# A two-layer hybrid decoder on one core: beta and alpha in fp32 on four column groups, paired small products, a fourth output tile ahead

## The chip, the core and the metric

The kernel runs on one core of one Trainium2 chip. The time is the device time of one execution in microseconds (us); the kernel before has a median of 2566.28 us over three runs (2564.98 to 2567.65). TensorE does matmuls and transposes and is called PE, VectorE is DVE, ScalarE is ACT, GpSimd is POOL, and SyncE (SP) issues the DMAs.

## The reference

The input x is 1024 tokens by 1024 channels in fp32. Two residual layers follow each other, each with a token mixer and a SwiGLU FFN, and a last RMSNorm. Cut to what matters here:

```python
def mixer_ab(h, ...):                     # layer 0
    qkv, z, beta_raw, alpha_raw, gate_b, gate_c, sc_in = split_cols(h @ w_in, AB_SPLITS)
    qkv = silu(causal_depthwise_conv(qkv, conv_w))
    beta = sigmoid(beta_raw)              # 4 heads
    g = -exp(a_log) * softplus(alpha_raw + dt_bias)
    o_a = gated_delta_rule(q, k, v, g, beta)      # chunked, triangular solve
    ...
def mixer_cd(h, ...):                     # layer 1
    o_c = hgrn2_recurrence(silu(hq), k_in, hi, log_f)    # chunked, per-channel decay
    for p, (window, dilation) in enumerate(((128, 1), (512, 4), (2048, 16))):
        o_p, lse_p = dilated_window_attention(sq[p], sk[p], sv[p], window, dilation)
    o_d = softmax-over-p weighted sum of o_p
    return concatenate([o_c, o_d]) @ w_out

for layer in range(2):
    h = h + mixer(rms_norm(h, norm_mix_g[layer]))
    h = h + (silu(hn @ w_gate) * (hn @ w_up)) @ w_down   # hn = rms_norm(h, norm_ffn_g)
return rms_norm(h, norm_final_g)
```

Beta and alpha are eight columns of `w_in` (four heads each), in the kernel the input `w_ba`.

## The kernel before

The state lies transposed: channels on the 128 partitions, 512 tokens (one of two halves) along the free side, so a tile of 128 channels by 512 tokens fills one PSUM bank. Three kinds of PSUM tiles share the eight banks: `psg` (2), `psu` (3) and `psm` (3). A dense product in fp32 accuracy is made from fp32r parts: `split` makes a high part on ACT and the rest on DVE, and `mm3` (L126 to L128) issues three matmuls for each block of 128 input channels: high by high, high by low, low by high. These three lines are most of the program; `hnh` and `hnl` are the two parts of the normed state, `w` the split weights in a ring of four units, loaded by `wload` through the tile `raw`.

The norm needs the mean square of each token. `tr.squares` and `tr.piece` make and add the squares (ACT and POOL, L183 and L187, name `acc`), `rms` sums them over partitions with small matmuls against ones (L199), and `spread` transposes the result over all partitions (L213). In layer 0 the projections run ahead of the norm: the matmuls use x times the norm gain, and each product is multiplied by `rb` (the spread reciprocal root) when it leaves PSUM (`lead`, L1208). Their order at the start is written by hand (`ordered` is a manual schedule for PE, DVE and ACT). After `ordered.close()` a list scheduler with priorities sets the order of each engine.

The rest of layer 0's first stage goes through eight units `u` (four heads by two halves). Between the four projections of a unit, `step(u, i)` runs one piece of other work as the string `plan[u]` says: `S` the next part of `scalars()`, `A` the first and `B` the second part of `chunk_mats` of an earlier unit, `x` nothing. Units without an entry use `"AxBx"`. `scalars()` makes beta and alpha: the raw weights `w_ba` are split into 16 fp32r columns, 32 matmuls (L1259) multiply them with `hnh` and `hnl`, DVE scales by `rb` into `bat` (L1262), and small matmuls with a selection matrix (`sel16`, L1264) add high and low parts and turn tokens onto partitions. Then follow the gates' cumulated sums and factors (`sca`). `chunk_mats` makes key by key and key by query products (L1429) and transposes (`nn`, L1442).

Layer 1's mixer is driven by two generators, `hg_chain` (HGRN2, eight units of `hgrn`) and `loc` (the attention). `tick(cost)` is called between the dense matmuls; it adds cost to what is due and runs a step of each when one is due. PE's and DVE's order is here the order of these calls. `hgrn` computes products inside chunks level by level; `blocks` (L1805) does the small levels in 32-wide column groups, L1855 the level of 32 and L1860 the level of 64, from `ms[3]` in two 64-wide groups.

A step of the attention (`local`) does the scores of step n, the flip (transpose of the exponentials, so that keys are on partitions) of step n−1 and the outputs of step n−2. For the third dilation (`self.p == 2`) a stream has only 64 positions; its scores (L2099) are 64-wide, DVE's reduce adds the mask and finds the maximum (L2106), ACT takes exponentials (L2107), the flip is L2113 into `dp` (two tiles, `diag`), the outputs L2139. `combine` weighs the three dilations on ACT and DVE (L2219, name `ol`), transposes on PE (L2226), and stores to `cat`, from where `joined` loads and splits it for the output projection.

`leading` computes parts of the first output tiles (input blocks 0 to 5 of 8) ahead, while the last attention steps run; `out_proj` finishes them, adds to the residual `h`, calls `tr.piece` for the next norm, and stores by `tr.save`.

Of the kernel before, what the change touches and what calls it, by code (L numbers as in the profile page):

```python
# [54 lines left out]
def hybrid_trunk_kernel(ctx: ExitStack, tc: tile.TileContext, x_t, w_all, w_down, w_ba, vecs, c_f, c_i, c_rope, out):  # L55
# [23 lines left out]
    dia32 = cf[:, C_DIA:C_DIA + 32]  # L79
    sel16 = cf[:16, C_SEL:C_SEL + 8]  # L80
    swam = cf[:, C_SWA:C_SWA + 256]
# [1079 lines left out]
    def out_proj(name, cat_d, tr, src, order, half, hp, lead=None):  # L1161
# [4 lines left out]
        for d0 in range(0, KT, 2):  # L1166
            w = ws.get(d0) or wload((name, d0), (name, d0 + 1))
            if d0 + 2 < KT:
                tr.load(half, src, range(d0 + 2, d0 + 4))
            for i in range(2):  # L1170
                if d0 + i in banks:
                    o = proj(wk(w, i), qs, rest, banks.pop(d0 + i), first=False)
                else:
                    o = proj(wk(w, i), qs, order, psg() if i else psu())
                h = tr.at(half, d0 + i)
                V.tensor_tensor(h, h, o, op=ADD)
                tr.piece(half, d0 + i)
                tr.save(half, d0 + i, hd[2 * layer][half])
                yield


    def mixer_ab(hn, rb, hp, tr, first, second, close):
        scr_n = dr.tile([4, 32, 32, 32], F32, name="scr_n")
# [27 lines left out]
        early = {}  # L1211
        a, b = range(KH), range(KH, KT)
        os3 = [proj(wk(wqk, i), hn[0], a, last=False) for i in range(2)]
        for i in range(2):
            proj(wk(wqk, i), hn[0], b, os3[i], first=False)
        os3.append(proj(wk(wvz, 0), hn[0], a, last=False))
        r = tr.rms(0)
# [6 lines left out]
        for which, o in enumerate(os3):  # L1224
            early[0, which] = lead(o, 0)
        second(1)
        early[1, 0] = proj(wk(wqk, 0), hn[1])
        early[1, 1] = proj(wk(wqk, 1), hn[1])
        second(2)
        early[1, 2] = proj(wk(wvz, 0), hn[1])  # L1230
        second(3)
        ordered.close()
        close()
        with ExitStack() as es:
# [8 lines left out]
            sca = {n: keep.tile([P, 8, 4], F32, name="s_" + n) for n in sc_names}  # L1243
            raw = fp.tile([P, KT, 8], F32, name="wba_raw")
            dma(raw, w_ba)
            na = keep.tile([P, 4], F32, name="na")
            wba = keep.tile([P, KT, 16], F32R, name="wba")
            split(wba[:, :, 0:8], wba[:, :, 8:16], raw)

            def scalars():  # L1250
                with ExitStack() as e2:
# [3 lines left out]
                    for half in range(NH):  # L1255
                        o = psu()
                        for k in range(KT):
                            for j in range(2):
                                T.matmul(o[:16, :], wba[:, k, :], hk(hn[half], j, k),  # L1259
                                         start=k == 0 and j == 0, stop=k == KT - 1 and j == 1)  # L1260
                        bat = bp.tile([16, HT], F32, tag="bat", name="bat", bufs=1)
                        V.tensor_tensor(bat, o[:16, :], rb[half][:16, :], op=MULT)  # L1262
                        for tt in range(4):
                            T.matmul(sel[:, half * 32 + tt * 8:half * 32 + tt * 8 + 8], bat[:, tt * P:(tt + 1) * P],  # L1264
                                     sel16, start=True, stop=True)
                    V.tensor_copy(ba, sel[:, 0:64].rearrange("p (c e) -> p c e", c=8))
# [95 lines left out]
            if True:  # L1362
# [84 lines left out]

                plan = {1: "xSSS", 2: "ABAB"}
                units, sc_ = [], scalars()
# [282 lines left out]
    def mixer_cd(hn, hp, pairs):  # L1732
# [7 lines left out]
        with ExitStack() as es:  # L1740
# [67 lines left out]
            def hgrn(u, states, ending):  # L1808
# [49 lines left out]
                for c in range(4):  # L1858
                    r, z = c % 2 * 64, 3 * P + c // 2 * 64
                    T.matmul(od[r:r + 64, z:z + 64], m[:, c * P:c * P + 64], m[:, c * P + 64:(c + 1) * P],  # L1860
                             start=True, stop=True, tile_position=(0, r))
                kt = hl("e4", (4, P), 3)
# [75 lines left out]
            def leading(tick):  # L1938
# [6 lines left out]
                ws[2] = wload(("cdo", 2), ("cdo", 3))  # L1945
                for d, bank in ((0, psg), (1, psg), (2, psu)):
                    o = banks[d] = bank()
                    for ks in ((0, 1), (2, 3), (4, 5)):
                        proj(wk(ws[d // 2 * 2], d % 2), qs, ks, o, first=ks[0] == 0, last=False)
                        tick(0.5)  # L1950
                while len(whole) < 4:
# [57 lines left out]
            class Attend:  # L2009
# [82 lines left out]

                def short_scores(self, n):
                    o = psm()
                    for b in range(2):
                        for e in range(2):
                            i = (2 * n + b) * 2 + e
                            t = slice(i * 32, (i + 1) * 32)
                            T.matmul(o[e * 64:(e + 1) * 64, (b + e) % 2 * 64:(b + e) % 2 * 64 + 64],  # L2099
                                     self.q.rearrange("p b t -> p (b t)")[:, i * 64:(i + 1) * 64],  # L2100
                                     self.k[:, :, t], start=True, stop=True, tile_position=(0, e * 64))
                    s = self.sc[n] = tl("sc", bufs=2)
                    for x in range(2):
                        z = slice(x * 64, (x + 1) * 64)
# [4 lines left out]

                def short_flip(self, n):  # L2110
                    s = self.sc.pop(n)
                    o = psm()
                    T.transpose(o[:, 0:P], s[:, 0:P], ident)  # L2113
                    pt = self.pt[n] = diag[n % 2]
                    copy = V.tensor_copy if n % 2 else S.copy
                    copy(pt[0:64, 0:256].rearrange("p (a t) -> p a t", t=64)[:, 0::3],
                         o[0:64, 0:P].rearrange("p (a t) -> p a t", t=64))
                    copy(pt[64:128, 128:192], o[64:128, 0:64])
                    copy(pt[64:128, 64:128], o[64:128, 64:128])

# [10 lines left out]

                def outputs(self, n):
                    pt = self.pt.pop(n)
                    if n % 2 == 0:
# [255 lines left out]
    tr.load(0, x_t[0], range(4, KT))  # L2390
    dma(cf[:, 0:P], c_f[:, 0:P])
    o = psg()
    for _ in range(16):
# [12 lines left out]
    for i in range(2):  # L2406
        arrived_half(i, *w1)
        for d in range(4 + 2 * i, 6 + 2 * i):
            scaled_in(0, d)
    w0, w1 = coming(("ab", 8)), coming(("ab", 12))  # L2410
    ring.tile([P, 24], F32, name="pad")
# [30 lines left out]
    for layer in range(2):  # L2442

        if layer == 0:
            mixer_ab(hn, rb, hp, tr, first, second, es.close)
        else:
# [63 lines left out]
def shape_constants():  # L2510
# [6 lines left out]
    cf[:, C_DIA:C_DIA + 32] = (i % 32)[:, None] == np.arange(32)[None, :]  # L2517
    cf[0:8, C_SEL:C_SEL + 8] = np.eye(8)
    cf[8:16, C_SEL:C_SEL + 8] = np.eye(8)
    cf[:, C_SWA:C_SWA + P] = np.where(i[None, :] >= i[:, None], 0.0, NEG)  # L2520
# [67 lines left out]
```

## Time and profile before

| | before |
|---|---|
| median of three runs | 2566.28 us (2564.98 to 2567.65) |
| profiled execution | 2559.81 us, span 2558.0 us |
| mean granted clock of PE | 0.997 |
| PE busy | 2537.2 us, 99% |
| DVE, ACT, POOL busy | 65%, 40%, 22% |
| share of PE in the chain that ended last | 71% |

The span goes from the first to the last instruction of the profiled execution, which took 1.8 us longer in all and is 6.5 us under the median. A matmul of 512 fp32r columns shows a duration near 0.39 us but starts every 0.227 us, since matmuls overlap in the pipeline; costs on PE are therefore read from start to start.

### The profile page before, as it was taken

The numbers are of one execution on the slowest core, as the hardware profiler recorded it, in microseconds if no ns is written. First come the engines' busy times: TensorE is split into PE (matmuls) and PEld (weight loads), VectorE is DVE, ScalarE is ACT, GpSimd is POOL, SyncE is SP. The second block draws the span as 40 slices with busy tenths as digits, with TensorE's granted clock in tenths as the row PEclk, the third lists the DMA queues.
The fourth block names the chain that finished last, engine by engine and source line by source line (L and its number), as shares of the span: only waits on it lengthen the run. The fifth ranks groups of instructions, "written<-read, shape, count | busy, mean of one in ns | idle before, by whom it ended". The sixth has DMA issues, their size and how long they took to land.

```text
span 2558.0 us, 37563 instructions
## 1 busy us (share of the span) xinstructions
PE 2537.2 (99%) x14076; PEld 2114.1 (83%) x14076; DVE 1661.4 (65%) x2819; ACT 1033.9 (40%) x1861; POOL 557.5 (22%) x461
## 2 busy tenths in 40 slices
PE   9999999999999999999999999999999999999998
PEld 7788888888888888887888888888888888888887
DVE  7886776685655665568677657655658565666554
ACT  5432123343333345344433446565535333334442
POOL 1110111334333310033333100000033333330001
PEclk9999999999999999999999999999999999999999
DMA  3434446424556588544234456767752455568853
GB/s 137 150 99 152 127 141 206 173 81 168 174 195 207 202 289 307 177 155 152 107 110 138 166 154 198 205 181 208 223 173 87 166 189 192 201 219 289 271 178 119
DMA packets 270070, 451.82 MB, mean 177 GB/s; under 512 B 33824, under 2 KB 125760, under 8 KB 269760
## 3 DMA queue, kind: packets, MB, share of 16 engines
q1 hardware_dynamic: 269888, 449.43, 53.9%
q8 instruction: 110, 1.80, 0.3%
q14 instruction: 72, 0.59, 0.1%
HBM read 307.16 MB, written 142.16 MB: 176 GB/s over the span
## 4 chain that ended last, share of the span: by engine, by line
PE 71%; DVE 7%; DMA 2%; ACT 1%; issue 1%; SPq 0%; POOL 0%; DVEq 0%; ACTq 0%; POOLq 0%
PE psu L126 12%; PE psu L128 12%; PE psu L127 12%; PE psg L126 6%; PE psg L128 6%; PE psg L127 6%; PE psm L127 4%; PE psm L128 4%; PE psm L126 4%; DVE h L223 1%; PE psm L2139 1%; DVE h L592 1%; PE psm L2081 1%; DVE w L289 1%; DMA raw<-in_dram 1%
## 5 line engine op out<-in xcount | busy, mean ns | idle before, releaser
L103 DVE TENSOR_TENSOR w<-raw,w 128x1024 fp32r<-128x1024 f32 (+1 forms) x325 | 385.3, 1188 | 134.3 <-ACT w L102 132.7
L102 ACT CAST w<-raw 128x1024 fp32r<-128x1024 f32 (+1 forms) x325 | 309.5, 954 | 269.1 <-PE psu L128 124.1
L126 PE MATMUL psu<-hnh,w 128*128 128x512 f32 x832 | 330.0, 397 | 0.4 <-ACT w L102 0.4
L128 PE MATMUL psu<-hnh,w 128*128 128x512 f32 x832 | 325.2, 391 | 0.0
L127 PE MATMUL psu<-hnl,w 128*128 128x512 f32 x832 | 324.5, 390 | 0.5 <-DVE hnl L2356 0.5
L187 POOL TENSOR_TENSOR acc<-acc,sq 128x512 f32<-128x512 f32 x52 | 78.6, 1512 | 514.3 <-ACT sq L183 514.2
L302 POOL TENSOR_TENSOR ws<-raw 128x512 f32<-128x512 f32 x54 | 88.2, 1634 | 443.6 <-DMA raw<-in_dram 217.4
L128 PEld LDWEIGHTS psu<-hnh,w 128*128 128x128 f32 x832 | 156.2, 188 | 33.7 <-DVE w L103 0.8
L127 PEld LDWEIGHTS psu<-hnl,w 128*128 128x128 f32 x832 | 156.4, 188 | 32.5 <-DVE hnl L2356 1.3
L126 PEld LDWEIGHTS psu<-hnh,w 128*128 128x128 f32 x832 | 156.3, 188 | 32.5 <-ACT w L102 0.5
L103 DVE TENSOR_TENSOR w<-ws,w 128x1024 fp32r<-128x1024 f32 x51 | 67.5, 1323 | 123.9 <-ACT w L102 123.8
L103 DVE TENSOR_TENSOR hidq<-hr,hidq 128x1024 fp32r<-128x1024 f32 x72 | 82.1, 1141 | 75.8 <-ACT hidq L102 75.7
L102 ACT CAST hidq<-hr 128x1024 fp32r<-128x1024 f32 x72 | 70.2, 979 | 102.7 <-DMA hr<-ts 60.6
L126 PE MATMUL psm<-hidq,w 128*128 128x512 f32 x264 | 102.7, 389 | 0.0
L127 PE MATMUL psm<-hidq,w 128*128 128x512 f32 x264 | 102.7, 389 | 0.0
L128 PE MATMUL psm<-hidq,w 128*128 128x512 f32 x264 | 102.7, 389 | 0.0
L308 POOL TENSOR_TENSOR raw<-raw,ws 128x512 f32<-128x512 f32 x51 | 69.2, 1356 | 134.1 <-DVE w L103 134.1
L126 PE MATMUL psu<-t4h,w 128*128 128x512 f32 x240 | 93.7, 390 | 0.5 <-ACT c L372 0.5
L128 PE MATMUL psu<-t4h,w 128*128 128x512 f32 x240 | 93.5, 390 | 0.0
L127 PE MATMUL psu<-t4l,w 128*128 128x512 f32 x240 | 93.4, 389 | 0.0
L126 PE MATMUL psu<-t3h,w 128*128 128x512 f32 x240 | 93.4, 389 | 0.0
L128 PE MATMUL psu<-t3h,w 128*128 128x512 f32 x240 | 93.4, 389 | 0.0
(503 smaller groups left out, 6556.0 us busy)
## 6 DMA issues: line engine op xcount, KB each, us to landing
raw<-in_dram SPq DMA_DIRECT2D x227, 512.0 KB, 4.0
sd<-in_dram SPq DMA_DIRECT2D x44, 512.0 KB, 4.0
hid<-hid SPq DMA_DIRECT2D x88, 256.0 KB, 2.9
sd<-sd SPq DMA_DIRECT2D x44, 512.0 KB, 3.3
hr<-ts SPq DMA_DIRECT2D x40, 512.0 KB, 4.8
raw<-sd SPq DMA_DIRECT2D x40, 512.0 KB, 4.5
hd<-h SPq DMA_DIRECT2D x48, 256.0 KB, 3.8
h<-hd SPq DMA_DIRECT2D x48, 256.0 KB, 5.3
```

The costliest lines, as they stand in the source:

```text
L102: S.copy(hi, src)
L103: eng.tensor_tensor(lo, src, hi.bitcast(F32), op=SUB)
L126: T.matmul(o, lh, rh, start=first and i == 0, stop=False, **kw)
L127: T.matmul(o, lh, rl, start=False, stop=False, **kw)
L128: T.matmul(o, ll, rh, start=False, stop=last and i == n - 1, **kw)
L187: (eng or G).tensor_tensor(a, a, q, op=ADD)
L223: V.scalar_tensor_tensor(h, h, vec[:, row + k:row + k + 1], pb, op0=MULT, op1=MULT)
L289: later(lambda: V.tensor_tensor(u[:, 1, c], src[:, c], u[:, 0, c].bitcast(F32), op=SUB))
L302: G.tensor_tensor(s[:, HT:], b[:, :HT], b[:, HT:], op=ADD)
L308: G.tensor_tensor(a[:, HT:], a[:, HT:], s[:, :HT], op=SUB)
L592: eng.tensor_tensor(dst, x, y, op=SUB)
L2081: T.matmul(o[:, z], self.block(self.q, j, 1), self.block(self.k, j, m), start=True, stop=True)
```

## The change

Six things change.

1. Beta and alpha. A tile `wba` of fp32 weights, 32 columns wide with eight used, is made at the start (POOL clears it, DVE multiplies the raw weights by the norm gain). `mixed(half, n, o)` issues four fp32 matmuls, each for another block of input channels and in another group of 32 columns, on x itself. Two calls do one half: 8 matmuls after the first 48 projection matmuls, 8 after the second column block of the second half. DVE scales into `bats`, 128 rows; the `sel` matmuls now sum over the groups as well. The 32 matmuls of L1259, the split and `bat` go.
2. `plan`: the scalars start one step earlier, the chunk halves move.
3. HGRN2: `ms[3]` in 32-wide pieces, eight matmuls in four column groups for four in two.
4. Third dilation: scores, flip and outputs of two steps together in every second step.
5. `leading`: a fourth output tile, with 0.4 for 0.5 per tick.
6. `tr.piece` in `out_proj` at a raised priority.

```diff
-    sel16 = cf[:16, C_SEL:C_SEL + 8]
+    sel32 = cf[:, C_SEL:C_SEL + 8]
...
-                tr.piece(half, d0 + i)
+                with tc.high_priority(offset=100):
+                    tr.piece(half, d0 + i)
...
+        bats = fp.tile([P, 2, HT], F32, tag="kq", name="bats", bufs=3)
         os3 = [proj(wk(wqk, i), hn[0], a, last=False) for i in range(2)]
+        oba = psg()
         for i in range(2):
             proj(wk(wqk, i), hn[0], b, os3[i], first=False)
+        for n in range(2):
+            mixed(0, n, oba)
...
+        V.tensor_tensor(bats[:, 0], oba, rb[0], op=MULT)
         second(1)
         early[1, 0] = proj(wk(wqk, 0), hn[1])
         early[1, 1] = proj(wk(wqk, 1), hn[1])
         second(2)
+        oba = psg()
+        for n in range(2):
+            mixed(1, n, oba)
         early[1, 2] = proj(wk(wvz, 0), hn[1])
         second(3)
+        V.tensor_tensor(bats[:, 1], oba, rb[1], op=MULT)
...
-                        o = psu()
-                        for k in range(KT):
-                            for j in range(2):
-                                T.matmul(o[:16, :], wba[:, k, :], hk(hn[half], j, k),
-                                         start=k == 0 and j == 0, stop=k == KT - 1 and j == 1)
-                        bat = bp.tile([16, HT], F32, tag="bat", name="bat", bufs=1)
-                        V.tensor_tensor(bat, o[:16, :], rb[half][:16, :], op=MULT)
                         for tt in range(4):
-                            T.matmul(sel[...], bat[:, tt * P:(tt + 1) * P], sel16, start=True, stop=True)
+                            T.matmul(sel[...], bats[:, half, tt * P:(tt + 1) * P], sel32, start=True, stop=True)
...
-                plan = {1: "xSSS", 2: "ABAB"}
+                plan = {1: "SxSS", 2: "AxxA", 3: "BABx", 4: "BAxB"}
...
                 m = ms[3]
                 for c in range(4):
-                    r, z = c % 2 * 64, 3 * P + c // 2 * 64
-                    T.matmul(od[r:r + 64, z:z + 64], m[:, c * P:c * P + 64], m[:, c * P + 64:(c + 1) * P],
-                             start=True, stop=True, tile_position=(0, r))
+                    z = 3 * P + c // 2 * 64
+                    for x in range(2):
+                        r = c % 2 * 64 + x * 32
+                        T.matmul(od[r:r + 32, z:z + 64], m[:, c * P + x * 32:c * P + x * 32 + 32],
+                                 m[:, c * P + 64:(c + 1) * P], start=True, stop=True, tile_position=(0, r))
...
-                for d, bank in ((0, psg), (1, psg), (2, psu)):
+                for d, bank in ((0, psg), (1, psg), (2, psu), (3, psu)):
                     o = banks[d] = bank()
                     for ks in ((0, 1), (2, 3), (4, 5)):
                         proj(wk(ws[d // 2 * 2], d % 2), qs, ks, o, first=ks[0] == 0, last=False)
-                        tick(0.5)
+                        tick(0.4)
...
                 def short_scores(self, n):
+                    if n % 2:
+                        return
                     o = psm()
-                    for b in range(2):
+                    for b in range(4):
...
                 def short_flip(self, n):
+                    if n % 2:
+                        return
...
+                    for y in range(2):
+                        T.transpose(o[:, y * P:y * P + P], s[:, y * P:y * P + P], ident)
...
                 def outputs(self, n):
+                    if self.p == 2:
+                        if n % 2 == 0:
+                            self.sums_out(n)
+                            self.sums_out(n + 1)
+                        return
+                    self.sums_out(n)
...
+    wba = hp.tile([P, KT, 32], F32, name="wba")
+    raw = hp.tile([P, KT, 8], F32, name="wba_raw")
+    dma(raw, w_ba)
+    G.memset(wba, 0.0)
+
+    def mixed(half, n, o):
+
+        for g in range(4):
+            T.matmul(o[g * 32:g * 32 + 32, :], wba[:, 4 * n + g, :], tr.at(half, 4 * n + g), start=n == 0, stop=n == 1,
+                     tile_position=(0, g * 32))
...
+    V.tensor_tensor(wba[:, :, 0:8], raw, vec[:, R_MIX:R_MIX + KT, None].to_broadcast([P, KT, 8]), op=MULT)
```

The order on PE at the places that the next section speaks of (line, operation, output and inputs, tile, count of equal neighbours). First the end of the beta and alpha block before, which stands behind the first chunk products of layer 0; `bat` is the scaled result, `cf` the constants with the selection matrix:

```order
L1259 MATMUL psu<-hnl,wba 16x512
L1259 MATMUL psu<-hnh,wba 16x512
L1264 MATMUL psm<-cf,bat 128x8 x4
L1259 MATMUL psu<-hnl,wba 16x512
L1259 MATMUL psu<-hnh,wba 16x512
L1259 MATMUL psu<-hnl,wba 16x512
L1259 MATMUL psu<-hnh,wba 16x512
L1259 MATMUL psu<-hnl,wba 16x512
L126 MATMUL psu<-hnh,w 128x512
```

After the change the first block of eight stands behind the 48th projection matmul, `h_98` and `h_99` being the tiles of x:

```order
L127 MATMUL psu<-hnl,w 128x512
L128 MATMUL psu<-hnh,w 128x512
L2416 MATMUL psg<-h_98,wba 32x512 x4
L2416 MATMUL psg<-h_99,wba 32x512 x4
L126 MATMUL psu<-hnh,w 128x512
```

and where the 32 matmuls were, only the spread of the norm (L213), the selection and the chunk products (L1428, before L1429) are left:

```order
L128 MATMUL psu<-hnh,w 128x512
L213 MATMUL psm<-cf,r_462 128x128 x4
L1263 MATMUL psm<-cf,bats 128x8 x4
L1428 MATMUL psg<-kq 128x256 x2
L1263 MATMUL psm<-cf,bats 128x8 x4
L1428 MATMUL psg<-kq 128x256 x2
L126 MATMUL psu<-hnh,w 128x512
```

So 16 fp32 matmuls stand earlier, and the projections follow the selection at once. Second, the transposes of `combine` in layer 1 (L2226 before, L2242 after, `ol` being the weighted output) among the output tiles computed ahead; before, 15 matmuls into `psg` stand between the last attention output and this place:

```order
L127 MATMUL psg<-hnl,w 128x512
L128 MATMUL psg<-hnh,w 128x512
L2226 MATMUL psu<-cf,ol 128x128 x4
L126 MATMUL psg<-hnh,w 128x512
L127 MATMUL psg<-hnl,w 128x512
```

After, there are 18, and the transposes are taken apart:

```order
L126 MATMUL psg<-hnh,w 128x512
L127 MATMUL psg<-hnl,w 128x512
L128 MATMUL psg<-hnh,w 128x512
L2242 MATMUL psu<-cf,ol 128x128 x2
L126 MATMUL psg<-hnh,w 128x512
L2242 MATMUL psu<-cf,ol 128x128
L127 MATMUL psg<-hnl,w 128x512
L2242 MATMUL psu<-cf,ol 128x128
L126 MATMUL psg<-hnh,w 128x512
```

They moved three matmuls later, and two matmuls stand between them. Third, a step of the third dilation with its flip (L2113, `sc` the exponentials) and its outputs (L2139, `dp` the transposed ones) beside HGRN2's levels (L1805), before:

```order
L2099 MATMUL psm<-k,q 64x64 x4
L2113 MATMUL psm<-cf,sc 128x128
L2139 MATMUL psm<-vp,dp_11663 128x128 x2
L1805 MATMUL psg<-q,kk 32x32 x16
L1805 MATMUL psg<-m 32x32 x48
```

After, an even step (scores L2102, outputs L2155):

```order
L128 MATMUL psu<-w,b22l 128x256
L2102 MATMUL psm<-k,q 64x64 x8
L2155 MATMUL psm<-vp,dp_11646 128x128 x2
L2155 MATMUL psm<-vp,dp_11648 128x128 x2
L1804 MATMUL psg<-q,kk 32x32 x16
```

and the flip in the odd step between:

```order
L127 MATMUL psu<-w,b22h 128x256
L128 MATMUL psu<-w,b22l 128x256
L2119 MATMUL psm<-cf,sc 128x128 x2
L126 MATMUL psu<-w,t1h 128x256
L127 MATMUL psu<-w,t1h 128x256
```

Scores and outputs now come twice as many at a time, and the flip stands by itself half way between.

More of the change, by code (lines that the diff above doesn't have):

```diff
@@ L1176, in out_proj, with mixer_ab @@
                 V.tensor_tensor(h, h, o, op=ADD)
-                tr.piece(half, d0 + i)
+                with tc.high_priority(offset=100):
+                    tr.piece(half, d0 + i)
                 tr.save(half, d0 + i, hd[2 * layer][half])
                 yield
-    def mixer_ab(hn, rb, hp, tr, first, second, close):
+    def mixer_ab(hn, rb, hp, tr, first, second, mixed, close):
         scr_n = dr.tile([4, 32, 32, 32], F32, name="scr_n")
@@ L1243, in mixer_ab @@
             sca = {n: keep.tile([P, 8, 4], F32, name="s_" + n) for n in sc_names}
-            raw = fp.tile([P, KT, 8], F32, name="wba_raw")
-            dma(raw, w_ba)
             na = keep.tile([P, 4], F32, name="na")
-            wba = keep.tile([P, KT, 16], F32R, name="wba")
-            split(wba[:, :, 0:8], wba[:, :, 8:16], raw)
             def scalars():
@@ L1255, in scalars @@
                     for half in range(NH):
-                        o = psu()
-                        for k in range(KT):
-                            for j in range(2):
-                                T.matmul(o[:16, :], wba[:, k, :], hk(hn[half], j, k),
-                                         start=k == 0 and j == 0, stop=k == KT - 1 and j == 1)
-                        bat = bp.tile([16, HT], F32, tag="bat", name="bat", bufs=1)
-                        V.tensor_tensor(bat, o[:16, :], rb[half][:16, :], op=MULT)
                         for tt in range(4):
-                            T.matmul(sel[:, half * 32 + tt * 8:half * 32 + tt * 8 + 8], bat[:, tt * P:(tt + 1) * P],
-                                     sel16, start=True, stop=True)
+                            T.matmul(sel[:, half * 32 + tt * 8:half * 32 + tt * 8 + 8], bats[:, half, tt * P:(tt + 1) * P],
+                                     sel32, start=True, stop=True)
                     V.tensor_copy(ba, sel[:, 0:64].rearrange("p (c e) -> p c e", c=8))
@@ L2093, in short_scores @@
                 def short_scores(self, n):
+                    if n % 2:
+                        return
                     o = psm()
-                    for b in range(2):
+                    for b in range(4):
                         for e in range(2):
                             i = (2 * n + b) * 2 + e
-                            t = slice(i * 32, (i + 1) * 32)
-                            T.matmul(o[e * 64:(e + 1) * 64, (b + e) % 2 * 64:(b + e) % 2 * 64 + 64],
+                            t, z = slice(i * 32, (i + 1) * 32), b // 2 * P + (b + e) % 2 * 64
+                            T.matmul(o[e * 64:(e + 1) * 64, z:z + 64],
                                      self.q.rearrange("p b t -> p (b t)")[:, i * 64:(i + 1) * 64],
@@ L2102, in short_scores @@
                     s = self.sc[n] = tl("sc", bufs=2)
-                    for x in range(2):
+                    for x in range(4):
                         z = slice(x * 64, (x + 1) * 64)
@@ L2110, in short_flip @@
                 def short_flip(self, n):
+                    if n % 2:
+                        return
                     s = self.sc.pop(n)
                     o = psm()
[L2113 to L2119, printed above, removed]
+                    for y in range(2):
+                        T.transpose(o[:, y * P:y * P + P], s[:, y * P:y * P + P], ident)
+                    for y in range(2):
+                        pt = self.pt[n + y] = diag[y]
+                        copy = V.tensor_copy if y else S.copy
+                        a = y * P
+                        copy(pt[0:64, 0:256].rearrange("p (a t) -> p a t", t=64)[:, 0::3],
+                             o[0:64, a:a + P].rearrange("p (a t) -> p a t", t=64))
+                        copy(pt[64:128, 128:192], o[64:128, a:a + 64])
+                        copy(pt[64:128, 64:128], o[64:128, a + 64:a + P])
                 def flip(self, n):
@@ L2132, in outputs, with sums_out @@
                 def outputs(self, n):
+                    if self.p == 2:
[4 more added lines that the diff above has]
+                    self.sums_out(n)
+                def sums_out(self, n):
                     pt = self.pt.pop(n)
@@ L2444, in hybrid_trunk_kernel @@
         if layer == 0:
-            mixer_ab(hn, rb, hp, tr, first, second, es.close)
+            mixer_ab(hn, rb, hp, tr, first, second, mixed, es.close)
         else:
@@ L2517, in shape_constants @@
     cf[:, C_DIA:C_DIA + 32] = (i % 32)[:, None] == np.arange(32)[None, :]
-    cf[0:8, C_SEL:C_SEL + 8] = np.eye(8)
-    cf[8:16, C_SEL:C_SEL + 8] = np.eye(8)
+    cf[:, C_SEL:C_SEL + 8] = (i % 32 < 8)[:, None] & ((i % 8)[:, None] == np.arange(8)[None, :])
     cf[:, C_SWA:C_SWA + P] = np.where(i[None, :] >= i[:, None], 0.0, NEG)
```

## Prediction

> **What bounds the kernel.** I read the engines' busy time, then the chain that ended last, then what TensorE (PE) waits for, then single stages. On the page the first row gives the span, the next each engine's busy time and share, the row of digits PE's busy tenths in 40 slices, PEclk its granted clock, and the last the chain's shares.
>
> ```profile
> span 2558.0 us, 37563 instructions
> PE 2537.2 (99%) x14076; PEld 2114.1 (83%) x14076; DVE 1661.4 (65%) x2819; ACT 1033.9 (40%) x1861; POOL 557.5 (22%) x461
> PE   9999999999999999999999999999999999999998
> PEclk9999999999999999999999999999999999999999
> PE 71%; DVE 7%; DMA 2%; ACT 1%; issue 1%; SPq 0%; POOL 0%; DVEq 0%; ACTq 0%; POOLq 0%
> ```
>
> PE is busy 99% of the span and in every slice, so the time is what PE has to issue plus its few waits. Of PE's waits these lie where the change works (in us: total, times, longest):
>
> ```profile
> PE psu L2226 <- DVE ol L2219: 2.0, 1, 2.0
> PE psm L199 <- POOL acc L187: 1.5, 1, 1.5
> PE psm L1442 <- DVE nn L1434: 1.4, 2, 1.2
> PE psm L2113 <- ACT dp L2119: 0.6, 1, 0.6
> PE psm L2113 <- ACT sc L2107: 0.4, 1, 0.4
> PE psu L1259 <- DVE xp L1208: 0.3, 1, 0.3
> ```
>
> Together they are 6.2 us, 0.24% of the span. The change can win PE work and such waits, no more.
>
> **Beta and alpha: what goes.** The timeline of PE (start, duration, line, names; the last bracket is idle time ahead):
>
> ```profile
> 51.95 0.41 PE L1259 MATMUL psu<-hnh,wba 128*16 128x512 f32 x1 [0.26 <-DVE xp L1208]
> ...
> 58.29 1.05 PE L1264 MATMUL psm<-cf,bat 16*128 16x8 f32 x8
> 59.27 0.40 PE L1259 MATMUL psu<-hnl,wba 128*16 128x512 f32 x1
> ...
> 60.20 0.39 PE L1259 MATMUL psu<-hnl,wba 128*16 128x512 f32 x1
> 60.43 0.39 PE L126 MATMUL psu<-hnh,w 128*128 128x512 f32 x1
> ```
>
> From 59.27 to 60.43 five matmuls start, so one costs 0.232 us of PE (its duration of 0.4 overlaps its neighbours'). The change removes 32: 7.4 us. Their wait of 0.26 is counted below.
>
> **What comes.** Two blocks of eight fp32 matmuls, 32 columns wide, 512 moving elements, in four column groups. No fp32 matmul of 512 stands in the trace; these are the nearest rows:
>
> ```profile
> 42.96 0.95 PE L199 MATMUL psm<-onesn,acc 128*128 128x1 f32 x8
> 43.77 0.49 PE L126 MATMUL psu<-hnh,w 128*128 128x512 f32 x1
> ...
> 49.79 1.89 PE L1429 MATMUL psg<-kq 128*128 128x256 f32 x8
> ...
> 1476.02 1.05 PE L1805 MATMUL psg<-m 128*32 128x32 f32 x96
> 1477.00 0.39 PE L126 MATMUL psu<-w,t1h 128*128 128x256 f32 x1
> ...
> 1487.36 0.43 PE L1855 MATMUL psg<-m 128*32 128x32 f32 x15
> 1487.72 0.45 PE L1860 MATMUL psg<-m 128*64 128x64 f32 x8
> 1488.10 0.50 PE L126 MATMUL psu<-w,hnh 128*128 128x512 f32 x1
> ```
>
> An fp32 matmul leaves two records (four matmuls of L1429 give x8). L1429, one after the other, takes at most 1.89/8 = 0.236 us a record of 256 elements, 0.92 ns an element. L1805, four groups of 32 columns, takes 0.98 us (1476.02 to 1477.00) for 96 records of 32 elements: 10.2 ns a record, 0.32 ns an element, 2.9 times as fast. Sixteen matmuls are 32 records of 512 elements: 15.1 us at L1429's rate, 5.2 at L1805's, 3.8 if all four groups overlap fully. I take 4.5, between the last two, since start-up weighs less in long records than in L1805's short ones. Net 4.5 − 7.4 = −2.9; the ends are −3.6 and +7.7.
>
> Here a page bears on it: the Trainium skill, "TensorE: Matmul & The Clock Gate", section "Measured speedup vs the span model", gives 2.38 times for three column groups of 32 at 512 elements; by that the blocks would take 15.1/2.38 = 6.3 us and this term would be −1.1. L1805's four groups at 2.9 are the measurement, and stay.
>
> The small `sel` matmuls go from 16 rows to 128. A block took 0.98 us (58.29 to 59.27); eight records on all rows with one element, L199's, take 0.81 (42.96 to 43.77). Two blocks: −0.3 (ends −0.4 and 0). The Pool memset, the gain on DVE and the raw weights' DMA, which moves ahead on SP's queue, lie in the first 19 us, ahead of the first block; it can only start after 48 projections, so I cost them at nothing; if the weights came late, PE would wait there by as much.
>
> **The new order in layer 0.** With beta and alpha ready sooner the plan puts the scalars one step earlier and the chunk halves in other steps. The rows that show what it is up against, PE at 88.89, then the stretches (span, then busy us and instruction counts of PE, weight loads, DVE, ACT, POOL), then a DVE group:
>
> ```profile
> 88.89 0.33 PE L1442 MATMUL psm<-cf,nn 128*128 128x128 f32 x1 [1.22 <-DVE nn L1434]
> ...
> 45.00:80.00 35.00, 34.61 (x167) 25.17 (x166) 31.72 (x72) 8.60 (x16) 4.74 (x9) 1.00 0.26 76
> 80.00:100.00 20.00, 18.46 (x93) 14.73 (x92) 16.75 (x49) 11.14 (x46) 3.81 (x5) 1.00 0.39 120
> ...
> L1262 DVE TENSOR_TENSOR bat<-psu,rb 16x512 f32<-16x512 f32 x2 | 1.4, 676 | 1.0 <-PE psu L1259 1.0
> ```
>
> PE waits 0.26 + 1.4 = 1.7 us there. In the new order 80 projections (18 us) stand between the `sel` matmuls and the first that needs a scalar, and the `nn` transposes come four at a time after more projections, so these waits can go. But DVE is busy 31.7 of 35 us; it is the next to be late. Two new halts of up to 0.5 us are possible, where PE first asks for the cumulated gate and where it asks for the first chunk's `nn`. DVE gets back the 1.0 us that L1262 waited for PE. I take −1.2, ends −1.7 and +0.5.
>
> **HGRN2's widest level.** A batch of L1860, eight records in two groups, takes 0.38 us (1487.72 to 1488.10). The 15 records before it start 0.36 earlier, though at 10.2 ns each they need 0.15: 0.2 us is the change of column width. Afterwards the batch is 16 records of 64 elements in the width already set, 0.33 us at 0.32 ns an element, 0.24 at four full groups, and the 0.2 is paid when full-width work follows or not at all. In place of 0.74 us for both that makes 0.39 to 0.68; I take a gain of 0.11 a batch, near the smaller end, because full-width work does follow. L1860's 64 records are 8 batches: −0.9 (ends −2.4 and 0).
>
> **The fourth output tile.** The wait of 2.0 us in full, and DVE's work that ends it:
>
> ```profile
> 1817.83 0.40 PE L128 MATMUL psg<-hnh,w 128*128 128x512 f32 x1
> 1820.19 1.26 PE L2226 MATMUL psu<-cf,ol 128*128 128x128 f32 x4 [1.95 <-DVE ol L2219]
> 1821.10 0.77 PE L126 MATMUL psg<-hnh,w 128*128 128x512 f32 x1
> 1821.67 0.63 PE L127 MATMUL psg<-hnl,w 128*128 128x512 f32 x1
> 1822.10 0.63 PE L128 MATMUL psg<-hnh,w 128*128 128x512 f32 x1
> ...
> 1818.64 2.28 DVE L2219 SCALAR_TENSOR_TENSOR ol<-cm,w,ol 128x128 f32<-128x128 f32 x8 [0.38 <-ACT ol L2221]
> ...
> 1811.00:1830.00 19.00, 16.84 (x79) 13.29 (x79) 12.88 (x52) 9.40 (x22) 0.00 (x0) 0.91 0.54 184
> ```
>
> DVE's eight steps of 0.285 give the first transposable block after the fifth (1820.07) and the last at 1820.92; that chain is the same after the change. PE now reaches the transposes 3 matmuls later (18 for 15) and puts two more between them, so by about 1821.0 it has done five more matmuls: 5 × 0.227 = 1.1 us gained. After the wait the next matmuls start 0.43 to 0.57 apart for 0.23, and the granted clock of the stretch is 0.91: about 1.1 us more. A wait of 1.3 in place of 1.95 may spare half of that. The fourth tile's own 18 matmuls run after the second group of transposes, where PE did not wait, so they only move. I take −1.7; ends −2.7 (nearly all) and 0 (the chain of DVE is late by as much as PE is early).
>
> **The third dilation in pairs.** The stretch with the tight place, then the times of its parts (min/median/max ns, first and last start):
>
> ```profile
> 1569.88 0.45 PE L2099 MATMUL psm<-k,q 128*64 128x64 f32 x8
> 1570.78 0.33 PE L2113 MATMUL psm<-cf,sc 128*128 128x128 f32 x1 [0.45 <-ACT sc L2107]
> ...
> L2099 PE MATMUL psm<-k,q x128: 222/222/270, 1548.6 to 1638.3; 128*64 128x64 f32 x128
> ...
> L2107 ACT ACTIVATE sc<-sc,stat x32: 331/347/362, 1550.4 to 1640.7; 128x64 f32<-128x64 f32 x32
> L2107 ACT ACTIVATION_READ_ACCUMULATOR sc<-sc,stat x32: 185/188/202, 1550.7 to 1641.0; 128x1 f32 x32
> ```
>
> Sixteen steps, 128/8, become eight of double work: eight changes of column width fewer, 8 × 0.2 = 1.6 us, of which I count half. Against it the transposes of an odd step wait for four exponentials for two: 2 × 0.54 = 1.1 us later. Steps start 6.0 us apart ((1638.3 − 1548.6)/15), mostly enough, but not where PE already waits. If two of eight flips wait 0.5 more, that is +1.0, less half of the 1.0 that L2113 waits now. Sum −0.3, ends −1.5 and +4 (every flip 0.7 late).
>
> **The priority of `tr.piece`.** POOL's order around L187's acc is the same, so the 1.5 us wait at L199 stays. SP issues the residual's stores and loads a few places earlier and the FFN's first weights later. I cost it at 0, ends −1 and +1 (a DMA or two late by its issue).
>
> **Sum.** −2.9 − 0.3 − 1.2 − 0.9 − 1.7 − 0.3 + 0 = −7.3 us. The profiled execution took 2559.81 us (span 2558.0 and 1.8 around it), 6.5 below the median of 2566.28 of the runs shown, so the sum is taken from both: 2552.5 for an execution like the profiled one, 2559.0 for the median. All the lower ends together would be −13.3, 2553, and need every part at its best; a measurement tells 0.2% here, 5.1 us, so under 2561.2 is faster and over 2571.4 slower.
>
> **Rivals.** (1) The groups do not overlap as L1805's do, because the second record of a matmul holds up the next group behind it: two at a time, 32 × 0.47/2 = 7.5 us, total −4.3, 2562.0; one at a time, 15.1, total +3.3, 2569.6. For it: L1860's two groups are the only other rows. Against it: L1805 has such pairs of records as well, and beats two at a time. The same page, "The mechanism", says that matmuls start in program order; by that rule the second record would hold the next group, which is the case of two at a time, and L1805's 2.9 speaks against it.
> (2) DVE sets the pace from 45 to 100 us: PE comes to the scalars and to `nn` earlier by what it saved and waits there by as much. The 4.4 us of the first three terms are given back: −2.9, 2563.4. For it: 31.7 of 35 us busy. Against it: the block of L1259 itself made DVE wait 1.0.
> (3) The paired flips come late, every one: four reduces and four exponentials do not fit into the step, PE waits 1.3 and then runs at the slower clock for 1.1, as after 1820: 8 × 2.4 = 19 us in place of −0.3, total +12, 2578. It decides for slower from 12.4/8 = 1.6 us a flip. Against it: 6.0 us a step, and only one wait of 0.4 for an exponential now.
>
> **Chances.** The forecast with its own range 2554.5 to 2561 has 0.58; (1) 0.13, (2) 0.19, (3) 0.06, and 0.04 for some other loss. A little of (1), where two at a time meets better bounds elsewhere, is faster too: faster 0.62, within 0.2% 0.29, slower 0.09. The range reaches to (2) and to most of (1): 2554 to 2567.
>
> **What would show it.** Right: blocks of 2.0 to 2.6 us at about 19 and 45 us in place of 7.4 at 52; no halt over 0.5 at the scalars and at the first `nn`; the wait for L2219's `ol` near 1.3; no L1860 switch; each flip's wait under 1. Wrong: a block over 3.5 us, PE waiting for DVE between 60 and 100 us by 3 or more, or waits for the exponentials that sum to over 8.

## The result and the profile after

| | before | changed |
|---|---|---|
| median of six runs each | 2564.51 us (2559.46 to 2567.65) | 2549.69 us (2547.55 to 2552.34) |
| ratio, 95% interval | 1 | 0.9944 (0.9931 to 0.9957) |
| profiled execution, span | 2559.81, 2558.0 us | 2547.55, 2545.7 us |

The kernel is faster by 14.8 us in the medians and by 12.3 us between the two profiled executions. 2559.0 was predicted, with 2554 as the lower end: the sign was right, the size half of what came. One of the eight runs of the layer-0 kernel below took 3616.69 us at a granted clock of 0.653 and is left out of its figures. The page of the changed kernel, span, busy time and granted clock, and then PE's waits:

```profile
span 2545.7 us, 37695 instructions
PE 2528.2 (99%) x14140; PEld 2111.4 (83%) x14140; DVE 1661.8 (65%) x2819; ACT 1032.9 (41%) x1860; POOL 561.4 (22%) x462
PEclk9999999999999999999999999999999999999999
```

```profile
PE psm L199 <- POOL acc L187: 1.8, 1, 1.8
...
PE psu L2242 <- DVE ol L2235: 0.9, 1, 0.9
PE psu L128 <- DVE w L103: 0.7, 2, 0.4
...
PE psm L2155 <- DVE dp L2127: 0.4, 1, 0.4
```

PE bounds as before. The waits for `nn`, for `xp` and for the exponentials are gone, that for `ol` is halved, and a new one for weights (L103) has come. Where the 12.3 us arise is read by laying PE's instructions of both profiles beside each other and following the difference of their start times. The changed kernel is 7.1 us ahead at the end of the projections of layer 0 (0.4 of it from before the first new block) and 6.9 when HGRN2 is under way (1500 us); 10.8 ahead at 1772 us (HGRN2 and the third dilation); 14.0 at 1841 us (transposes of `combine`); and 12.4 from 1919 us to the end.

PE's timeline at the blocks of beta and alpha, at the selection, at HGRN2's last levels, at a double step of the third dilation, and at the transposes:

```profile
19.07 1.92 PE L2416 MATMUL psg<-h,wba 128*32 128x512 f32 x16
20.93 0.51 PE L126 MATMUL psu<-hnh,w 128*128 128x512 f32 x1
...
45.23 1.92 PE L2416 MATMUL psg<-h,wba 128*32 128x512 f32 x16
47.08 0.50 PE L126 MATMUL psu<-hnh,w 128*128 128x512 f32 x1
...
53.09 0.96 PE L1263 MATMUL psm<-cf,bats 128*128 128x8 f32 x8
53.90 1.11 PE L1428 MATMUL psg<-kq 128*128 128x256 f32 x4
54.87 1.06 PE L1263 MATMUL psm<-cf,bats 128*128 128x8 f32 x8
55.78 1.11 PE L1428 MATMUL psg<-kq 128*128 128x256 f32 x4
...
1480.61 0.38 PE L1854 MATMUL psg<-m 128*32 128x32 f32 x12
...
1480.86 0.41 PE L1861 MATMUL psg<-m 128*32 128x64 f32 x14
1481.19 0.50 PE L126 MATMUL psu<-w,hnh 128*128 128x512 f32 x1
...
1562.60 0.69 PE L2102 MATMUL psm<-k,q 128*64 128x64 f32 x16
1563.21 1.30 PE L2155 MATMUL psm<-vp,dp 128*128 128x128 f32 x8
1564.27 0.48 PE L126 MATMUL psu<-w,hnh 128*128 128x512 f32 x1
...
1808.38 0.59 PE L2242 MATMUL psu<-cf,ol 128*128 128x128 f32 x2 [0.86 <-DVE ol L2235]
1808.72 0.48 PE L126 MATMUL psg<-hnh,w 128*128 128x512 f32 x1
...
1809.72 0.40 PE L127 MATMUL psg<-hnl,w 128*128 128x512 f32 x1
1809.95 0.39 PE L128 MATMUL psg<-hnh,w 128*128 128x512 f32 x1
```

A block of 16 records takes 1.86 us (19.07 to 20.93) and 1.85: 3.7 us for both in place of 7.4. The level of 64 now follows the level of 32 with no pause; the matmuls behind the transposes start 0.23 us apart, not 0.43.

### The profile page after: what moved, and what is told of

The parts are those of the page before. It is cut to its first block, busy times and chain, and to the rows that moved or that the text cites. A ratio compares the mean times of both kernels' runs of the same rounds, so it can differ in the third digit from the quotient of the medians.

```text
span 2545.7 us, 37695 instructions
## 1 busy us (share of the span) xinstructions
PE 2528.2 (99%) x14140; PEld 2111.4 (83%) x14140; DVE 1661.8 (65%) x2819; ACT 1032.9 (41%) x1860; POOL 561.4 (22%) x462
## 4 chain that ended last, share of the span: by engine, by line
PE 72%; DVE 7%; DMA 2%; ACT 1%; issue 1%; POOL 0%; SPq 0%; DVEq 0%; ACTq 0%; POOLq 0%
PE psu L126 13%; PE psu L128 12%; PE psu L127 12%; PE psg L126 6%; PE psg L128 6%; PE psg L127 6%; PE psm L126 4%; PE psm L128 4%; PE psm L127 4%; DVE h L223 1%; PE psm L2155 1%; DVE h L592 1%; PE psm L2082 1%; DVE w L289 1%; PE psg L1804 1%
## 5 line engine op out<-in xcount | busy, mean ns | idle before, releaser
L103 DVE TENSOR_TENSOR w<-raw,w 128x1024 fp32r<-128x1024 f32 (+1 forms) x325 | 384.8, 1186 | 132.2 <-ACT w L102 131.5
L126 PE MATMUL psu<-hnh,w 128*128 128x512 f32 x840 | 333.8, 397 | 0.0
L128 PE MATMUL psu<-hnh,w 128*128 128x512 f32 x840 | 328.4, 391 | 0.7 <-DVE w L103 0.7
L103 DVE TENSOR_TENSOR w<-ws,w 128x1024 fp32r<-128x1024 f32 x51 | 67.4, 1322 | 125.7 <-ACT w L102 125.7
L103 DVE TENSOR_TENSOR hidq<-hr,hidq 128x1024 fp32r<-128x1024 f32 x72 | 82.2, 1143 | 76.3 <-ACT hidq L102 76.0
```

The lines of the kernel that those rows point to most:

```text
L103: eng.tensor_tensor(lo, src, hi.bitcast(F32), op=SUB)
L126: T.matmul(o, lh, rh, start=first and i == 0, stop=False, **kw)
L128: T.matmul(o, ll, rh, start=False, stop=last and i == n - 1, **kw)
```

## The experiments

Ten kernels were run, the changed one again among them. Six were executed once only, with the profiler: one group 2563.69 us, the old plan 2557.70, single steps 2551.06, two groups of 64 2556.28, three tiles 2551.84, no raised priority 2551.34. Runs of one kernel mostly spread by 5 to 8 us, so these six are read by their profiles and not by their times. Where one profile is compared with another, the difference of PE's start times at one place of the program is given.

**Layer 0 alone.** Parts 1 and 2 on the kernel before: `mixed`, `bats`, `sel32` and the new `plan`, nothing else.

> The kernel before with only parts 1 and 2 of the change (beta and alpha in fp32 on four column groups, and the plan). Theory A (the gain is spread over the program as PE's offsets between the two profiles say): the projections up to 232 us are 6.9 us ahead of the kernel before and nothing after that changes, so about -7 us, ratio 0.9973. Theory B (the stages share the gain, the early lead is what keeps layer 1 from its waits): more than -9 us. Theory C (DVE takes part of it back later in layer 0): less than -4 us.

Median 2558.03 against 2565.83 us, ratio 0.9973 (0.9962 to 0.9984): 7 to 8 us, as theory A said. In its profile PE is 6.0 to 7.0 us ahead from 181 to 1550 us. About half of the whole gain is made in the first 230 us. Behind 1700 us, where this kernel's code is that of the kernel before, its lead still grows from 5.9 to 9.1 us (1919 us): 1.0 of it at the transposes, which the kernel before passed at a lower clock. So single stages of two profiles can differ by 1 us or more with nothing changed in them.

**One column group for four.**

```diff
...
-            T.matmul(o[g * 32:g * 32 + 32, :], wba[:, 4 * n + g, :], tr.at(half, 4 * n + g), start=n == 0, stop=n == 1,
-                     tile_position=(0, g * 32))
+            T.matmul(o[0:32, :], wba[:, 4 * n + g, :], tr.at(half, 4 * n + g), start=n == 0 and g == 0,
+                     stop=n == 1 and g == 3, tile_position=(0, 0))
```

> The changed kernel with all 16 fp32 matmuls of beta and alpha in one column group of 32 in place of four; the result of each half then stands in 32 rows, which DVE and the selection read. Theory A (the four groups overlap fully; in the changed kernel a block of 16 records takes 1.86 us): a block takes four times the matmul part, 6.9 to 7.6 us, so both blocks cost 10 to 11.5 us more and the first 232 us are that much longer. Theory B (what saves the time is fp32 with half as many matmuls, not the groups): a block takes 2 to 4 us and the time hardly changes.

PE's timeline of this kernel:

```profile
18.72 7.05 PE L2416 MATMUL psg<-h,wba 128*32 128x512 f32 x16
25.71 0.50 PE L126 MATMUL psu<-hnh,w 128*128 128x512 f32 x1
...
65.67 1.48 PE L1263 MATMUL psm<-cf,bats 32*128 32x8 f32 x8 [0.50 <-DVE bats L1241]
...
69.38 0.63 PE L127 MATMUL psu<-hnl,w 128*128 128x512 f32 x1
69.81 0.63 PE L128 MATMUL psu<-hnh,w 128*128 128x512 f32 x1
```

A block takes 6.99 us for 1.86, 3.8 times as long, 0.44 us a record. Both blocks cost 10.3 us more, and PE is 9.9 us later behind the second. This is theory A. Further on it loses another 4.2 us between 65 and 73 us: a wait of 0.50 us for DVE's `bats`, and right behind it matmuls at half clock (0.43 us apart for 0.23). So the groups overlap almost fully and are what saves the time: one after the other, the 16 matmuls (14.0 us) would cost nearly twice the 32 that they replace.

**The old plan.** `plan = {1: "xSSS", 2: "ABAB"}` in the changed kernel.

> The changed kernel with the old plan table, so that beta and alpha come early and the scalars and chunk halves stay in their old steps. Theory A (the early blocks give 4 us, and the plan what is left of 6.9 us by taking away PE's waits of 1.7 us and some insertions among the dense matmuls): the halt at the first nn transpose is 0.5 to 1.3 us again, and the projections up to 225 us are 1 to 3 us later than in the changed kernel. Theory B (the waits go with the block of 32 matmuls alone, and the plan does nothing): within 0.5 us of the changed kernel at 225 us.

```profile
PE psm L1441 <- DVE nn L1433: 2.5, 2, 1.5
```

PE is 2.8 us later at 225 us, and 2.5 of it are these two waits for `nn` (1.02 and 1.50 us). Theory A, at its upper end. With the early blocks and the old plan PE waits more than the 1.4 us of the kernel before: what the blocks save there goes partly into waiting for DVE, and the plan gets it back. PE is still 4.2 us ahead of the kernel before at 225 us.

**Single steps of the third dilation** (`short_scores`, `short_flip` and `outputs` as before, the rest changed).

> The changed kernel with the third dilation's steps single again (part 4 undone). Theory A (each change of the width of the column groups and each insertion among the dense matmuls costs PE, and half as many steps halve it): PE's stretch of the third dilation, from its first scores to its last outputs, is 2.0 to 2.6 us longer than in the changed kernel, of which at most 1.3 are waits for ACT. Theory B (the 2.9 us came from the waits for ACT alone, or from HGRN2's 32-wide level): under 1.4 us longer, and the wait rows say all of it.

```profile
PE psm L2114 <- ACT dp L2120: 0.6, 1, 0.6
PE psm L2114 <- ACT sc L2108: 0.5, 1, 0.5
PE psm L2140 <- ACT ol L2148: 0.3, 1, 0.3
```

Added over all steps, from the start of the scores, flips and outputs to the next instruction of another kind, they take 17.0 us of PE here, 14.7 in the changed kernel and 16.9 in the kernel before. The 2.3 us between the first two are 0.9 of waits (1.3 here by the timeline, 0.4 in the changed kernel, for `dp`) and 1.4 of work. Theory A: the work alone is more than the waits. The other profiles bear this out: less the waits inside the steps, it is 14.0 to 14.4 us in all nine with paired steps and 15.6 to 15.7 in the three with single ones.

**HGRN2's widest level in two groups of 64.**

> The changed kernel with HGRN2's widest level in two groups of 64 again (part 3 undone). Theory A (each batch loses 0.15 to 0.2 us, the change of width and the lesser overlap): level 32 and level 64 together take 0.74 to 0.77 us again for 0.57, eight times, so 1.2 to 1.6 us in all. Theory B (the switch is paid anyway when full-width work follows): below 0.6 us in all.

From the first record of level 32 to the full-width work behind level 64, the eight batches take 0.74 to 0.77 us each, 0.60 in the changed kernel: 0.155 × 8 = 1.2 us, theory A's lower end. PE's timeline in this kernel, to be laid beside 1480.61 above (each batch's first record, up to 0.03 us earlier, stands in a row of its own):

```profile
1482.33 0.43 PE L1854 MATMUL psg<-m 128*32 128x32 f32 x15
1482.69 0.45 PE L1859 MATMUL psg<-m 128*64 128x64 f32 x8
1483.07 0.50 PE L126 MATMUL psu<-w,hnh 128*128 128x512 f32 x1
```

This execution is 8.8 us behind the changed kernel's from 1919 us on. Most of that lies elsewhere: it has a wait of 1.7 us for `u` (L1629) in layer 0 and one of 3.2 for `acc`, with half clock behind it.

**Three output tiles ahead** and 0.5 per tick.

> The changed kernel with three output tiles ahead and tick 0.5 (part 5 undone). Theory A (the gain of 3.1 us at the transposes of combine is a wait shortened from 1.95 to 0.86 us and the slower clock after it gone): the wait for DVE's ol is 1.8 to 2.1 us again, the five matmuls after it start 0.37 to 0.57 us apart, and the stretch is 2.9 to 3.3 us longer. Theory B (PE simply came there at another time relative to DVE because of the other parts): the wait stays below 1.2 us and the matmuls after it start 0.23 us apart.

```profile
1810.17 1.11 PE L2242 MATMUL psu<-cf,ol 128*128 128x128 f32 x4 [1.38 <-DVE ol L2235]
1811.04 0.48 PE L126 MATMUL psg<-hnh,w 128*128 128x512 f32 x1
1811.36 0.40 PE L127 MATMUL psg<-hnl,w 128*128 128x512 f32 x1
1811.59 0.39 PE L128 MATMUL psg<-hnh,w 128*128 128x512 f32 x1
```

Neither theory as written: the wait lies between them, and the clock stays. Over all profiles the wait at this place is 1.95 (before), 1.96 (layer 0 alone) and 1.38 with three tiles, mean 1.76; with four tiles (the last experiment aside) it is 0.86, 0.6, 0.9, 1.1, 1.3, 1.4, 1.2 and 1.15, mean 1.06. The difference of 0.7 us fits the three matmuls (0.68 us) that the fourth tile puts ahead, though the two ranges touch at 1.38. In the layer-0 kernel the wait of 1.96 us is followed by matmuls 0.23 us apart, so the slow matmuls of the kernel before, 1 us, came in that execution and need not. Nor does the gain last in these two executions: with three tiles PE is 2.9 us behind the changed kernel at 1841 us (2.0 of it from before the transposes) and level with it from 1906 us on, since the changed kernel's two late weight units don't come here and half clock behind the column sums lasts 3.4 us for 6.8.

**No raised priority** (`tr.piece` as before).

> The changed kernel without the raised priority of the squares (part 6 undone). Theory A (the order of loads on SP that part 6 brings makes two weight units late, which are the new waits of 0.39 and 0.33 us for DVE's w after the transposes of combine): those waits go, and PE is 0.5 to 1.2 us earlier at the end of the output projection. Theory B (those waits come from the other parts, since PE arrives earlier): they stay at 0.3 or more each.

```profile
PE psu L126 <- ACT w L102: 1.4, 2, 1.0
...
PE psm L199 <- POOL acc L187: 1.1, 1, 1.1
...
PE psu L128 <- DVE w L103: 0.5, 1, 0.5
```

The waits for weights do not go; one of 1.0 us for ACT and one of 0.5 for DVE stand in their place. Theory B as far as that: the priority is not their cause. The wait for `acc` was 1.1 in place of 1.8 in this one execution, so part 6 has shown no gain.

**The changed kernel again.**

> The changed kernel itself, once more, with another profile. Theory A (executions of one kernel differ by a phase of half clock at the very end, 31 or 32 matmuls and 3.2 to 3.4 us, that some have and some not, and by small waits for DMAs): the median lies between 2548 and 2552 us, ratio 0.994 to 0.996, and the profile is that of the first one within 0.5 us up to 390 us and within 3 us at 2530 us, with or without the phase at the end. Theory B (the first profile was a lucky one throughout): the layer-0 stretch or the third dilation differs by over 1 us.

Median 2550.30 against 2566.21 us on that chip, ratio 0.9941 (0.9928 to 0.9953), and the profile stays within 1.2 us of the first one everywhere (within 0.3 up to 390 us, 1.0 to 1.2 ahead from 397 to 1560 us, 0.6 behind at the end). Theory A.

**One sum of squares on DVE.** Not a part of the change, but of the wait that it left largest:

```diff
-                    tr.piece(half, d0 + i)
+                    tr.piece(half, d0 + i, V if layer and half and d0 + i == KT - 2 else None)
```

> The changed kernel with one sum of squares, the seventh of the second half in layer 1's output projection, on DVE in place of POOL, where it stands behind four operations of the FFN's weights. Theory A (that queue is the 1.80 us wait, and the wait brings the slow clock of the 11 matmuls after it, 2.3 us): the wait before the column sums falls below 1.0 us and the matmuls after it start 0.23 us apart; the time falls by 2.5 to 4.2 us, ratio to the kernel before about 0.993. Theory B (ACT's square or the next wait takes its place, or the slow clock comes from the small matmuls and not from the wait): the wait falls by less than 1 us or the matmuls stay 0.43 us apart, and under 1.5 us are won.

PE's timeline of the changed kernel, and then of this one:

```profile
1898.55 1.05 PE L199 MATMUL psm<-onesn,acc 128*128 128x1 f32 x8 [1.80 <-POOL acc L187]
1899.47 1.46 PE L199 MATMUL psm<-onesn,sq 128*128 128x1 f32 x8
1900.78 0.78 PE L126 MATMUL psg<-hnh,w 128*128 128x512 f32 x1
1901.36 0.63 PE L127 MATMUL psg<-hnl,w 128*128 128x512 f32 x1
1901.78 0.63 PE L128 MATMUL psg<-hnh,w 128*128 128x512 f32 x1
```

```profile
1900.47 0.94 PE L199 MATMUL psm<-onesn,acc 128*128 128x1 f32 x8
1901.28 1.03 PE L199 MATMUL psm<-onesn,sq 128*128 128x1 f32 x8
1902.17 0.49 PE L126 MATMUL psg<-hnh,w 128*128 128x512 f32 x1
1902.50 0.40 PE L127 MATMUL psg<-hnl,w 128*128 128x512 f32 x1
1902.73 0.40 PE L128 MATMUL psg<-hnh,w 128*128 128x512 f32 x1
```

The wait is gone and the clock stays; PE gains 5.2 us on the changed kernel between 1896 and 1908 us. The median is 2546.97 against 2565.59, ratio 0.9926 (0.9912 to 0.9939); the interval overlaps those of the changed kernel (0.9931 to 0.9957 and 0.9928 to 0.9953), so the gain is shown at this place and not in the whole time. Theory A at this place, with more than it said, since the column sums themselves ran slower behind the wait too (1.46 for 1.03 us).

**Transposes later.** The kernel with the sum on DVE, and:

```diff
-                        tick(0.4)
+                        tick(0.45)
...
                 yield
                 yield
+                if h == 3:
+                    yield
                 o = psu()
```

> The changed kernel with the sum of squares on DVE as in the experiment on it, one step more between the weighing and the transposes of the last head (h == 3), and 0.45 for 0.4 per tick, so that 24 in place of 18 matmuls stand ahead of the first transposes. Theory A (that wait, 0.9 to 1.4 us, is the distance to DVE's chain of ol): it falls below 0.3 us and the time by 0.8 to 1.4 us against the kernel with the sum on DVE. Theory B (the step moved makes the loads of cat late for the output projection): a wait for hnl or ACT's hnh of the same size comes right after.

Median 2542.89 against 2566.21 us, ratio 0.9911 (0.9896 to 0.9926), 7.4 us under the changed kernel in the same comparison, with the two intervals apart: the two last steps together beat both kernels. No wait for `ol` is left among PE's waits of 0.3 us and over, and the one for `hnl` is 0.3 us as in the changed kernel: theory A for the wait. Against the kernel with the sum on DVE, timed on another chip, the ratios differ by 0.0015, 4 us, but their intervals overlap, so that the step's own gain is not settled beyond the wait removed.

## Why the prediction was wrong in size

- **Sum.** Between the profiled executions 7.3 us were predicted and 12.3 found. The forecast stood on the right mechanisms, and no rival decided; what failed is the size of its terms. Two were far too small: the order in layer 0 (−1.2 for about −2.9 measured) and the third dilation (−0.3 for −2.2), in both, halts were charged that did not come (0.5 and 1.0 us), and PE's work beside the waits was counted too low or not at all. On top of the sum, the step from the profiled execution to the median failed (last point).
- **Beta and alpha, −2.9.** Measured −3.7. The step "I take 4.5, between the last two" was the error: the groups overlap fully, 3.7 us for 3.8 at four full groups. L1805's short records took 0.32 ns an element, these long ones 0.23; a start-up in each record would explain it and was not measured by itself. Rival 1 falls: 6.99 against 1.86 us.
- **Selection, −0.3.** The first block takes 0.81 us (53.09 to 53.90), the second 0.91: −0.24.
- **Order in layer 0, −1.2.** Layer 0 gave 6.7 to 7.0 us (two profiles) for 4.4. All 1.7 us of waits went (2.0 with those under 0.15 us) and neither new halt came. The rest, about 1 us, is spread over PE's work, and its cause stays open: from 19 to 232 us there are 21 places where small matmuls stand between dense ones, 23 before, and the first dense matmul behind them costs 2.7 us in all in both. The plan is worth 2.8 us by its own experiment, since without it the early blocks would have lengthened the waits. Rival 2 names that effect rightly; it holds in part with the old plan (2.5 us of waits for DVE) and not with the new.
- **HGRN2's level, −0.9.** −1.2: the pause of 0.2 was dropped almost whole. The lower end in the prediction, −2.4, doesn't follow from its own figures: 8 × (0.74 − 0.39) is 2.8.
- **Third dilation, −0.3.** −2.2 (16.9 to 14.7 us): 1.3 of work for the 0.8 counted, and 0.9 of waits. The step "if two of eight flips wait 0.5 more" did not come, and the waits that were to go by half went nearly all: the flip stands by itself half a step later, after the exponentials have ended. Rival 3 falls with it.
- **Fourth tile, −1.7.** 3.1 us between the two profiles. Its own part, the 0.7 us of wait, was sized rightly; the rest was the slow clock of that one execution (1.0 us) and where PE met DVE's chain, which was luck as far as the forecast goes.
- **Priority, 0.** No gain shown. Between 1841 and 1919 us 1.6 us are given back: 1.3 at two late weight units (0.7 of it waiting, the rest in the start of the matmuls behind) and 0.3 more at `acc`. Without the priority PE waited for weights as well, so it is not their cause.
- **Profile to median.** I carried the 6.5 us between the profiled execution and the median over to the changed kernel. There it was 2.1 us. That alone puts the forecast 4.3 us too high, nearly as much as the sum did (5.0). For the kernel before, the six runs give 4.7 in place of 6.5. The last section has the likeliest cause, which is not shown.

## What to carry to other kernels

Where PE is the bound, price every place at which it changes between kinds of matmuls, and every wait together with the clock after it: together they gave more than the 3.7 us of work that beta and alpha saved (changes of kind 1.2 and 1.3 us, waits 2.0, 0.9 and 0.7). A table that moves steps is to be priced with the change that makes them early, not by itself: here the early blocks without the new plan gave part of their gain back. And take the ends of a sum from rows whose size is that of the new work, or lean to the end that long instructions favour.

## What was not expected of the hardware

A profiled execution can hold a stretch of half clock near its end with no wait ahead of it. PE's timeline and the stretch (the number right behind the five engines' busy times is the granted clock) in the kernel with three tiles, then the same stretch in the changed kernel:

```profile
2533.07 0.27 PE L128 MATMUL psu<-hidq,w 128*128 128x128 f32 x1
2533.18 0.33 PE L126 MATMUL psu<-hidq,w 128*128 128x128 f32 x1
2533.31 0.42 PE L127 MATMUL psu<-hidq,w 128*128 128x128 f32 x1
2533.52 0.41 PE L128 MATMUL psu<-hidq,w 128*128 128x128 f32 x1
...
2534.00:2541.00 7.00, 7.00 (x35) 7.00 (x33) 2.84 (x5) 0.71 (x2) 0.55 (x1) 0.50 0.42 150
```

```profile
2534.00:2537.00 3.00, 3.00 (x29) 3.00 (x29) 2.48 (x4) 0.71 (x2) 0.44 (x1) 1.00 0.29 104
```

The narrow matmuls of 128 elements start 0.21 us apart in place of 0.11, which costs 3.2 to 3.4 us on them, and 4.0 to 4.4 in all: from the first of them to the end of the span it takes 20.7 to 21.1 us in place of 16.7 to 16.8. It is in five of the twelve profiles (layer 0 alone, old plan, three tiles, no priority, sum on DVE), not in those of the kernel before, of the changed kernel, or of the last one. It would make up most of the 5 to 8 us by which runs of one kernel mostly spread, and, if the kernel before has it more often, part of the difference between 12.3 us by profiles and 14.8 by medians: of its 30 timed runs beside the experiments 19 had a mean granted clock of 0.996 or less, of the changed kernel's eleven 3. Compared at like clock, the medians differ by 13.7 us (runs at 0.997 or more, 2562.59 and 2548.91) and by 13.2 (the others, 2566.22 and 2552.98).

What sets it off was not tried, but the kept traces say when it can come. In each of the twelve the granted clock steps only at times that lie whole multiples of 3.413 us apart, on a raster that starts at another place in each execution; in the kernel before these are 1819.84, 1823.25, 1912.00, 1918.82 and 2553.70 us. Where this raster falls sorts the profiles without exception: in the five with the stretch one of its times lies 0.9 to 1.3 us behind the first narrow matmul, in the seven others 2.1 to 3.1 us behind it, and the work there is the same in all. So in these executions the place of the raster, and not the kernel, goes with the stretch; that it decides was not tried, and what a section of the raster must hold for the clock to fall stays open. A wait isn't it, and a wait alone doesn't decide either: 1.95 us before the transposes were followed by slow matmuls, 1.96 us in the layer-0 kernel were not, while each wait of 1.1 us or more before the column sums was, in every profile that has one.
